# Hybrid encoder step: the FFN's up projection by seven products of block sums instead of eight block products, on equal token groups

## The chip, the cores and the metric

The kernel runs on one core of a Trainium2 chip. The metric is the device time of one execution in microseconds (us). A core has TensorE (PE; PEld is its weight load), VectorE (DVE), ScalarE (ACT) and GpSimd (POOL), all of which read and write the on-chip memory SBUF; TensorE writes its sums to PSUM, which the others read. SyncE (SP) issues the DMAs.

## What is computed

One layer of a streaming encoder over 2048 prompt tokens and 32 sample tokens, model width 1024, in float32:

```python
n = rmsnorm(x, g_mix);  z = n @ w_in                  # attention and gated linear attention (GLA)
h = x + concat(attention, gla) @ w_out                # output projection
y = h + relu(rmsnorm(h, g_ffn) @ w_up)^2 @ w_down     # FFN: w_up 1024 x 4096, w_down 4096 x 1024
```

The change concerns the last line, above all `rmsnorm(h) @ w_up`.

## The kernel before

Three phases follow one another: attention, GLA, and from about 780 us on `ffn_phase` with the output projection and the FFN. Activations lie feature-major: 128 features on the partitions, tokens along the free axis.

Each large product runs in a split precision: a float32 matrix is written as a pair of float32r parts, high and low (`h`, `l`), and `mm3` issues three matmuls for one block product (high by high, high by low, low by high). The high part is written by ScalarE as a rounded copy, the low one is the difference, taken by VectorE (of activations) or GpSimd (of weights, L198).

The FFN takes the tokens in three pieces of two groups: 288 + 256 tokens, then 384 + 384 twice. For each piece:

1. The output projection `op` of both groups, 8 blocks of 128 features f, each 8 x 3 matmuls (`project_out`). VectorE adds it to the residual stream `y` (L1048), ScalarE squares the sum (L1050) and VectorE adds the squares up in `acc` (L1052). With group 1's blocks, group 0's normed input is split: ScalarE writes `h0h` (L1038), VectorE `h0l` (L1039); group 1's `h1h`, `h1l` follow within block 0. `token_scale` is a task woven into TensorE's order: one matmul `ss` with a matrix of ones sums `acc` over the partitions, then VectorE computes 1/sqrt on a full 128 x N tile `rb` (L993, L170 to L175).
2. 16 blocks b of 256 FFN columns. `weights(b)` loads and splits four tiles of 128x1024: two of w_up (`wu`), two of w_down (`wd`). `up(b, gi)` computes two halves mi of 128 columns, each 8 feature blocks x 3 = 24 matmuls (tile `up`); on the result VectorE takes relu and the scale (L1083, PSUM to `rr`), ScalarE squares it into `uh` (L1085), VectorE squares it too (L1086) and takes the low part `ul` (L1087). `down(b, gi)` has 8 features x 2 halves x 3 = 48 matmuls (tile `dn`), and VectorE adds each of the 8 results to `y` (L1104). So a block has 96 up and 96 down matmuls. The order on TensorE is up(b, 0), down(b-1, 1), up(b, 1), down(b, 0): group 1 runs half a block behind, and while u of one group is being finished, TensorE works on the other. The u tiles have two buffers.

TensorE's program order is the order of the code (`_pe` chains the instructions; `tick` weaves spawned tasks in). The orders on the other engines are the tile scheduler's.

Of the kernel before, what the change touches and what calls it, by code (L numbers as in the profile page):

```python
# [9 lines left out]
F32 = mybir.dt.float32  # L10
# [18 lines left out]
class Builder:  # L29
    def __init__(self, ctx, tc, a, o, nt=NT, ffn=True):  # L30
# [19 lines left out]
        # the tensor engine's program order: GEMMs, with tasks woven in  # L50
# [6 lines left out]
    # tile index nt stands for the sample's 32 tokens  # L57
# [12 lines left out]
    def tok_pair(self, name, n):  # L70
        """A float32r pair [P, 8, n]."""
        return tuple(
            self.tok.tile([P, KB * 288], F32R, tag="tok", name=f"{name}{x}")[:, : KB * n].rearrange(
                "p (k t) -> p k t", k=KB
            )
            for x in "hl"
        )
# [7 lines left out]
    # ------------------------------------------------ tensor engine: order and tasks  # L85
# [6 lines left out]
    def mm(self, out, lhsT, rhs, start, stop):  # L92
        n = 1
        for d in rhs.shape[1:]:
            n *= d
        m = 1
        for d in lhsT.shape[1:]:
            m *= d
        if rhs.dtype == F32R:
            ns = max(n / 2.4 + 2.5, 0.835 * m)  # L100
        else:
            ns = 4 * n / 2.4 + 5
            if m <= 64:  # beside one in the other half of the columns
                ns /= 2
        self._pe(self.T.matmul(out, lhsT, rhs, start=start, stop=stop), ns)  # L105
# [5 lines left out]
    def table(self, *args, **kw):  # L111
        """An activation of the GLA phase: in program order, so that its functions change tables seldom."""
# [25 lines left out]
    def finish(self, *tasks):  # L138
        """Run the tasks (all of them, without arguments) to their ends."""
# [11 lines left out]
    def gemm(self, ps, lh, ll, rh, rl):  # L151
        """ps = (lh + ll).T @ (rh + rl) over 8 blocks of the contraction."""
# [25 lines left out]
    def rms(self, xt, sq, r, name):  # L178
        """rsqrt(mean(xt^2) + eps), row by row; sq takes the squares."""
# [5 lines left out]
    def split_weight(self, src, hi, lo, hi_eng="act", lo_eng="pool", parts=1):  # L185
        """Load a piece [128, k, c] of a weight, k * c <= 1024, and write it as a float32r pair."""
# [13 lines left out]
    def cols_pair(self, w, c0, name, engs=(("act", "pool"), ("act", "pool")), k0=0, nk=KB):  # L200
        """Rows 128*k0 : 128*(k0+nk), columns c0 : c0+2048/nk of a [P, 8, *] weight view as a float32r pair."""
# [19 lines left out]
    # ------------------------------------------------ attention  # L221
    def attention_phase(self):
# [3 lines left out]
        with ExitStack() as ctx:  # L226
# [17 lines left out]
            def front(t, xT=None):  # L244
                """x * g, feature-major, as a float32r pair."""
# [21 lines left out]
            def scales(t, x=None):  # L267
                """1 / rms of each token, by which its products are scaled."""
# [4 lines left out]
            def store(t):  # L273
                """The pair and the scales, for the GLA phase."""
# [11 lines left out]
            S.activation(self.rstd[:, :1], self.ones[:, :1], AF.Square)  # L286
# [6 lines left out]
            # k, v and, beside them, the forget gate's low-rank part  # L293
# [10 lines left out]
            gq, gk, snk, snks = self.gq, self.gk, self.snk, self.snks  # L304
# [52 lines left out]
            def project_gate(t):  # L357
                """The gate's projection, kept for the GLA phase."""
# [7 lines left out]
            def softmax_tail(rsum, negm, snk_b, n, name):  # L366
                """1 / (rsum + exp(sink - max))"""
# [7 lines left out]
            def transposed_qk(t, qk, kn, ca):  # L375
# [7 lines left out]
                caT = wk.tile([16, P], F32, tag="caT", name=f"caT_{t}")  # L383
# [4 lines left out]
            def attend_sample(qk, kn, v, ca):  # L388
# [48 lines left out]
                aT = self.const.tile([P, 4, P], F32, tag="mo", name="aT_s", bufs=2)  # L437
# [3 lines left out]
            def attend(t, qk, kn, v, ca):  # L441
# [22 lines left out]
                for ch in range(2):  # L464
# [46 lines left out]
                for ch in range(2):  # L511
                    ops = []
                    for vt, a0, m in parts[ch]:
# [5 lines left out]
                        else:  # L519
                            # both heads' 64 keys on the partitions  # L520
# [15 lines left out]
                aT = self.const.tile([P, 4, P], F32, tag="mo", name=f"aT_{t}", bufs=2)  # L536
# [6 lines left out]
            # the first two tiles go together, so that there is work while the weights come in  # L543
# [25 lines left out]
            # the GLA phase's first projections run beside the last tiles' attention  # L569
# [11 lines left out]
    # ------------------------------------------------ gated linear attention  # L581
    GLA_ENG = (("act", "pool"), ("dve", "dve"))

    def load_gla_consts(self):
        a, c, Q, V = self.a, self.mid, self.Q, self.V
        ct = lambda shape, name, dt=F32: c.tile(shape, dt, tag=name, name=name, bufs=1)
        masks, d0 = ct([P, 7, 32], "masks", I32), ct([P, 544], "d0")
# [39 lines left out]
    def decay(self, h, tail=None):  # L627
        """The running sums of log sigmoid(ca @ w_alpha + b_alpha), restarted at each tile."""
# [4 lines left out]
        resets = d0[:, :288] if h == 0 else d0[:, 288:]  # L633
# [23 lines left out]
    def gla_phase(self):  # L657
        tc, a, V, S, G, Q = self.tc, self.a, self.V, self.S, self.G, self.Q
        nt = self.nt
        with ExitStack() as ctx:  # L660
# [3 lines left out]
            masks, d0, wal, bal, one, ones = self.gla_consts  # L664
            St = {}
# [13 lines left out]
            def reach(n, s):  # L679
                """Run the n-th tile's task to the end of a stage (1: diagonal, 2: scores, 3: outputs, 4: all)."""  # L680
# [4 lines left out]
            def gates(h):  # L685
                """silu(gate) * g_gla_out"""
                for t in halves[h]:
# [6 lines left out]
                    G.tensor_tensor(out=gv, in0=gv, in1=self.ggla[:r].unsqueeze(1).broadcast_to([r, 4, P]), op=ALU.mult)  # L694
# [54 lines left out]
            def gla_tile(n, t, off, qg, kg, cc):  # L749
# [55 lines left out]
                # the diagonal of the scores  # L805
# [16 lines left out]
                # level by level, the pairs that a block's middle parts  # L822
# [42 lines left out]
                # outputs, token by token, and the state after these tokens  # L865
# [29 lines left out]
                # norm per head, gate, transpose  # L895
# [16 lines left out]
                gT = self.const.tile([P, 4, P], F32, tag="mo", name=f"gT_{t}", bufs=2)  # L912
# [16 lines left out]
    # ------------------------------------------------ output projection and FFN  # L929
# [4 lines left out]
    def load_mix(self, g, pair):  # L934
        """The attention's and the GLA's outputs for tiles g, feature-major, as a float32r pair."""
        off = 0
        for t in g:
            r = self.rows(t)
            m = self.io_tile(f"m_{t}")[:, : KB * r].rearrange("p (k t) -> p k t", k=KB)
            self.Q.dma_start(m, self.mixT[t])  # L940
            hi, lo = (x[:, :, off : off + r] for x in pair)
            self.S.activation(hi, m, AF.Copy)
            self.V.tensor_tensor(out=lo, in0=m, in1=hi.bitcast(F32), op=ALU.subtract)
            off += r
        return off

    def project_out(self, f, N, pair, wo, name):
        """Features 128*f : 128*(f+1) of the output projection."""
# [3 lines left out]
        self.gemm(ps, lambda kb: w(kb, 0), lambda kb: w(kb, 1), lambda kb: pair[0][:, kb, :N], lambda kb: pair[1][:, kb, :N])  # L952
        return ps

    def prepare_ffn(self, part):
# [5 lines left out]
        # the first tiles' output projection runs beside the last tiles' GLA  # L961
        if part < 3:
            self.mix.append(self.tok_pair(f"m{part - 1}", 288))
            self.load_mix(self.pieces[0][part - 1], self.mix[-1])
            return
        self.wo += self.load_wout(0, (1,), (("act", "pool"), ("dve", "dve")))
        self.op0, N = [], sum(self.rows(t) for t in self.pieces[0][0])
# [6 lines left out]

    def ffn_phase(self, pieces):
# [279 lines left out]
```

## Time and profile before

| | |
|---|---|
| median of three runs | 2415.68 us (2412.44 to 2417.94) |
| the profiled execution: span | 2416.1 us, mean granted TensorE clock 0.982 |
| TensorE busy | 2318.7 us, 14981 matmuls |
| VectorE, ScalarE, GpSimd busy | 1543.2, 717.9, 746.2 us |

The profiled execution's own time is its span, from the first to the last instruction. Busy times of different engines overlap; which of them sets the time is read from the chain of waits that ended last. In a group's row of the profile stand the line, the engine, what is written from what, the shape and the count, then busy us and mean ns of one, then the idle time before it and its releaser.

### The profile page before, as it was taken

The page shows a single profiled execution, that of the slowest core. Times are in us where ns is not written, and L with a number is a line of the kernel's source. Part 1 is how long each engine was busy: PE and PEld are TensorE (multiplying, and loading weights), DVE is VectorE, ACT ScalarE, POOL GpSimd, SP SyncE. Part 2 cuts the span into 40 slices and gives each one's busy share as a digit, 9 for nine tenths or more (in the row PEclk, how much of TensorE's full clock was granted, in tenths as well). Part 3 has the DMA queues.
Part 4 walks back from the last instruction along what each step waited for, and adds up shares of the span by engine and source line. Part 5 has one row for each costly group of instructions (what it writes and reads, how often), then busy time and mean ns, then how long its engine had stood idle before and what let it go on. Part 6 is the DMA issues. An engine that isn't in the chain of part 4 may idle for free.

```text
span 2416.1 us, 37655 instructions
## 1 busy us (share of the span) xinstructions
PE 2318.7 (96%) x14981; PEld 2183.3 (90%) x14981; DVE 1543.2 (64%) x3403; ACT 717.9 (30%) x1397; POOL 746.2 (31%) x636
## 2 busy tenths in 40 slices
PE   6999999889978899999999999999999999999999
PEld 5777777777868899999999999999999999999999
DVE  6766666999997866666656555554565655555554
ACT  3554444545443322222323111111122311111110
POOL 3222235332430343434313223332231322333220
PEclk9999999999989899999999999999999999999999
DMA  9764564223224332323432122222252212221211
GB/s 212 149 132 107 124 170 123 62 66 99 66 77 135 97 105 71 106 71 119 153 97 71 61 62 70 70 62 61 80 167 84 73 56 68 70 71 56 60 33 53
DMA packets 199279, 221.55 MB, mean 92 GB/s; under 512 B 18064, under 2 KB 163040, under 8 KB 199104
## 3 DMA queue, kind: packets, MB, share of 16 engines
q1 hardware_dynamic: 199104, 219.15, 32.7%
q8 instruction: 118, 1.93, 0.4%
q14 instruction: 57, 0.47, 0.1%
HBM read 180.21 MB, written 38.91 MB: 91 GB/s over the span
## 4 chain that ended last, share of the span: by engine, by line
PE 79%; DVE 13%; DMA 4%; issue 2%; ACT 2%; POOL 1%; SPq 0%; DVEq 0%; POOLq 0%; ACTq 0%
PE dn L105 29%; PE up L105 29%; PE op L105 7%; PE zq L105 4%; PE zr L105 3%; DVE Qb L793 3%; PE zkv L105 2%; DVE AT L858 1%; PE O L105 1%; DVE E L799 1%; DMA xT1a<-in_xT_prompt 1%; PE S L105 1%; PE zv L105 1%; DMA stage<-in_w_in 1%; DMA nTl<-nT_0l 1%
## 5 line engine op out<-in xcount | busy, mean ns | idle before, releaser
L1104 DVE TENSOR_TENSOR y<-y,dn 128x384 f32<-128x384 f32 (+2 forms) x768 | 379.5, 511 | 157.7 <-PE dn L105 155.5
L1083 DVE SCALAR_TENSOR_TENSOR rr<-up,rb 128x384 f32<-128x384 f32 (+1 forms) x192 | 99.4, 518 | 385.5 <-PE up L105 385.1
L1085 ACT ACTIVATE uh<-rr 128x384 fp32r<-128x384 f32 (+1 forms) x192 | 93.7, 489 | 716.6 <-DVE rr L1083 716.6
L1086 DVE TENSOR_TENSOR rr<-rr 128x384 f32<-128x384 f32 (+1 forms) x192 | 173.5, 905 | 66.1 <-ACT uh L1085 65.7
L1087 DVE TENSOR_TENSOR ul<-rr,uh 128x384 fp32r<-128x384 f32 (+1 forms) x192 | 175.4, 915 | 3.2
L793 DVE TENSOR_TENSOR Qb<-qg,E 64x128 f32<-64x128 f32 (+1 forms) x234 | 86.2, 368 | 7.2 <-ACT E L113 4.0
L694 POOL TENSOR_TENSOR g<-g,packed 128x512 f32<-128x512 f32 (+1 forms) x17 | 22.7, 1340 | 168.5 <-ACT g L113 168.5
L858 DVE COPY_PREDICATED AT<-masks,A 64x128 f32<-64x128 int32 (+1 forms) x197 | 67.5, 342 | 8.4 <-ACT AT L851 3.4
L494 ACT ACTIVATE P<-S,negm 128x192 f32<-128x192 f32 (+2 forms) x128 | 51.5, 417 | 52.2 <-DVE negm L489 35.4
L1048 DVE TENSOR_TENSOR y<-y,op 128x384 f32<-128x384 f32 (+2 forms) x48 | 24.0, 512 | 67.3 <-PE op L105 67.3
L783 POOL TENSOR_TENSOR E<-cc 128x128 f32<-128x128 f32 (+1 forms) x117 | 48.5, 414 | 17.0 <-PE A L105 8.9
L784 POOL TENSOR_TENSOR E<-cc 128x128 f32<-128x128 f32 (+1 forms) x117 | 51.9, 444 | 0.0
L488 DVE TENSOR_REDUCE mx<-S 128x2 f32<-128x384 f32 (+2 forms) x64 | 32.5, 533 | 24.3 <-PE S L105 24.2
L507 POOL TENSOR_TENSOR P<-P,es 128x512 f32<-128x512 f32 x15 | 15.6, 1041 | 98.1 <-DVE es L372 42.0
L198 POOL TENSOR_TENSOR wu_0l<-stage,wu_0h 128x1024 fp32r<-128x1024 f32 x3 | 7.5, 2483 | 121.5 <-ACT wu_0h L194 121.5
L105 PE MATMUL go<-Sp,Qc 128*128 128x256 f32 x60 | 22.0, 454 | 23.5 <-DVE Sp L891 23.5
L1050 ACT ACTIVATE sq<-y 128x384 f32<-128x384 f32 (+2 forms) x42 | 20.5, 490 | 80.2 <-DVE y L1048 74.2
L799 DVE TENSOR_TENSOR E<-E,kg 128x1024 f32<-128x1024 f32 (+2 forms) x34 | 40.4, 1205 | 0.1
L113 ACT ACTIVATE E<-E 128x1024 f32<-128x1024 f32 (+2 forms) x34 | 33.7, 1009 | 18.5 <-POOL E L774 12.2
L105 PEld LDWEIGHTS A<-Qb,E 128*64 128x64 f32 (+1 forms) x852 | 32.2, 149 | 6.9 <-issue 3.1
L815 ACT ACTIVATE AT<-packed,dg 128x128 f32<-128x128 f32 (+1 forms) x68 | 21.3, 384 | 57.4 <-DVE dg L813 57.4
L105 PE MATMUL dn<-uh,wd_0h 128*128 128x384 f32 (+2 forms) x96 | 33.2, 345 | 5.4 <-ACT uh L1085 5.4
(1147 smaller groups left out, 8651.3 us busy)
## 6 DMA issues: line engine op xcount, KB each, us to landing
stage<-in_w_up SPq DMA_DIRECT2D x96, 512.0 KB, 3.8
stage<-in_w_down SPq DMA_DIRECT2D x96, 512.0 KB, 3.6
stage<-in_w_out SPq DMA_DIRECT2D x24, 512.0 KB, 4.7
xT1a<-in_xT_prompt SPq DMA_DIRECT2D x16, 512.0 KB, 6.7
stage<-in_w_in SPq DMA_DIRECT2D x16, 512.0 KB, 13.1
x1a<-in_x_prompt SPq DMA_DIRECT2D x16, 512.0 KB, 5.1
m<-mixT SPq DMA_DIRECT2D x16, 512.0 KB, 4.8
y<-in_xT_prompt SPq DMA_DIRECT2D x16, 512.0 KB, 6.7
```

The costliest lines, as they stand in the source:

```text
L105: self._pe(self.T.matmul(out, lhsT, rhs, start=start, stop=stop), ns)
L494: S.activation(Pt[:, u, :n], sp[:, jp], AF.Exp, bias=negm[:, ch, u : u + 1], scale=0.125, accum_out=rsum[:, ch, u : u + 1],)
L783: G.tensor_tensor(out=e5[:, :, :, 0, :], in0=ref, in1=c5[:, :, :, 0, :], op=ALU.subtract)
L784: G.tensor_tensor(out=e5[:, :, :, 1, :], in0=c5[:, :, :, 1, :], in1=ref, op=ALU.subtract)
L793: (G if li % 4 < 0 else V).tensor_tensor(out=Qt[hp, li, :, hh, : L // 2].rearrange("q p (n m) -> q p n m", m=m), in0=q[hp].rearrange("q p ...
L799: V.tensor_tensor(out=E[:, :ng, :, :L], in0=E[:, :ng, :, :L], in1=k.unsqueeze(1).broadcast_to([P, ng, 2, L]), op=ALU.mult)
L858: V.copy_predicated(dst, mk.unsqueeze(1).broadcast_to([L // nh, 4, w // m, m]), src)
L1083: V.scalar_tensor_tensor(out=rr, in0=ps, scalar=0.0, in1=rbs[gi], op0=ALU.max, op1=ALU.mult)
L1085: last_s = S.activation(uhs, rr, AF.Square)
L1086: V.tensor_tensor(out=rr, in0=rr, in1=rr, op=ALU.mult)
L1087: last_v = V.tensor_tensor(out=ul[:, mi, :], in0=rr, in1=uhs.bitcast(F32), op=ALU.subtract)
L1104: V.tensor_tensor(out=yg[:, f, :], in0=yg[:, f, :], in1=ps, op=ALU.add)
```

## The change

**Pieces.** The groups of a piece get equal size: 320 + 320 tokens, then 360 + 360 twice. The groups no longer fall on multiples of 128 tokens, so their loads and stores are cut in more parts.

**Up projection.** For a block of 256 columns and a piece's two groups, the product is seen as 2 x 2 blocks: A by halves of the columns and of the 1024 features (4 feature blocks each), B by halves of the features and by group. Seven products of sums (Winograd's form of Strassen's scheme) give the four results: P0 = A11 B11, P1 = A12 B21, P2 = S1 T1, P3 = S2 T2, P4 = S3 T3, P5 = A22 T4, P6 = S4 B22. Each is 4 x 3 = 12 matmuls, 84 a block. The results are c0 = P0 + P1, and with r2 = P0 + P3, r0 = r2 + P4: c1 = r0 - P5, r0 + r1 (r1 = P2), and r2 + r1 + P6. VectorE forms them; `finished` then takes relu and scale (VectorE), the square and its rounded copy (ScalarE) and the low part (VectorE). `uh0`, `ul0` and `uh1`, `ul1` are the two column halves of group 0, 2 and 3 those of group 1.

**Weight sums.** `up_weights` forms S1 to S4 on GpSimd: with the seven low parts, eleven GpSimd operations of 128x512 and, for w_down, two of 128x1024 a block, where there were four of 128x1024. ScalarE writes seven high parts of 128x512 and two of 128x1024.

**Token sums.** At a piece's start `combine` forms T1, T2, T4 beside group 1's output projection, and T3 and B22 follow. Every sum and its pair must be there before its product in block 0.

**Order.** up(b) has all seven products, then down(b, 0), which starts with the first halves of four features, then down(b, 1). Nothing runs half a block behind. u, r0 to r2, the T and B tiles have one buffer.

**Token scale.** `token_scale` now sums into a small tile (120 x 3 or 80 x 4), takes the rsqrt on that, and spreads it by matmuls `rb` to `cb`. In TensorE's order `ss` of group 1 stands ahead of P1 of block 0, and its `rb` ahead of P2.

```diff
-        if nt == 16:
-            self.pieces = [[[0, 1, nt], [2, 3]], [[4, 5, 6], [7, 8, 9]], [[10, 11, 12], [13, 14, 15]]]
...
+        for n in (320, 360, 360):
...
+            def up_weights(b, name):
...
+                names = ("A11", "A12", "S1", "S2", "S4", "S3", "A22")
...
+                def pair(x, src):
+                    h, l = ws[x]
+                    S.activation(h, src, AF.Copy)
+                    G.tensor_tensor(out=l, in0=src, in1=f32(h), op=ALU.subtract)
...
+                pair("A11", A(1, 1))
+                pair("A12", A(1, 2))
+                pair("A22", A(2, 2))
+                tt(A(2, 2), A(2, 1), A(2, 2), ALU.add)
+                tt(A(2, 1), A(1, 1), A(2, 1), ALU.subtract)
+                tt(A(1, 1), A(2, 2), A(1, 1), ALU.subtract)
+                pair("S1", A(2, 2))
+                tt(A(1, 2), A(1, 2), A(1, 1), ALU.subtract)
+                pair("S2", A(1, 1))
+                pair("S3", A(2, 1))
+                pair("S4", A(1, 2))
...
+                def finished(i, x):
+                    V.scalar_tensor_tensor(out=x, in0=x, scalar=0.0, in1=cb[i // 2], op0=ALU.max, op1=ALU.mult)
+                    S.activation(x, x, AF.Square)
+                    S.activation(uh[i], x, AF.Copy)
+                    V.tensor_tensor(out=ul[i], in0=x, in1=f32(uh[i]), op=ALU.subtract)
...
+                    S.activation(r0, product(0, "A11", "B11"), AF.Copy)
+                    ps = product(1, "A12", "B21")
+                    if b == 0:
+                        self.finish(*tasks)
+                    tt(c0, ps, r0)
+                    finished(0, c0)
+                    S.activation(r1, product(2, "S1", "T1"), AF.Copy)
+                    ps = product(3, "S2", "T2")
+                    tt(r2, ps, r0)
+                    ps = product(4, "S3", "T3")
+                    tt(r0, ps, r2)
+                    tt(r2, r2, r1)
+                    ps = product(5, "A22", "T4")
+                    tt(c1, r0, ps, ALU.subtract)
+                    finished(1, c1)
+                    ps = product(6, "S4", "B22")
+                    tt(r0, r0, r1)
+                    finished(3, r0)
+                    tt(r2, ps, r2)
+                    finished(2, r2)
...
+                for k in range(H):
+                    f = H + k
+                    t0 = (r[1], r[2], tmp[:, :N], tmp[:, N : 2 * N])[k]
+                    S.activation(t0, y[1][:, k, :], AF.Copy, scale=g(k))
+                    V.scalar_tensor_tensor(out=t0, in0=y[1][:, f, :], scalar=g(f), in1=t0, op0=ALU.mult, op1=ALU.subtract)
+                    split("T3", k, t0)
+                for k in range(H):
+                    scaled("B22", k, 1, H + k)
...
-                for b in range(NF):
-                    last_s, last_v = up(b, 0)
...
-                        down(b - 1, 1)
...
-                    up(b, 1)
...
-                    down(b, 0)
...
+                for b in range(NF):
+                    last = b + 1 == NF
+                    up(b)
...
+                    down(b, 0, 4)
...
+                    down(b, 1)
```

What moves on the engines shows at three places. In the rows, `dn_1_7_0_0` is down's tile for piece 1, block 7, group 0, feature 0, the number behind a name is the buffer's, and the bracket names the engines or DMA queues that are waited for. First VectorE in the middle of the second piece, block 7, as group 0's u is finished, before:

```order
L1083 SCALAR_TENSOR_TENSOR rr_1_7_0_0_15916<-up_1_7_0_0_15891,rb1_0_13734 128x384 [waits PE_49]
L1086 TENSOR_TENSOR rr_1_7_0_0_15916<-rr_1_7_0_0_15916 128x384 [waits Activation_49]
L1087 TENSOR_TENSOR ul_1_7_0_15890<-rr_1_7_0_0_15916,uh_1_7_0_15889 128x384 [waits DVE_49]
L1083 SCALAR_TENSOR_TENSOR rr_1_7_0_1_15946<-up_1_7_0_1_15921,rb1_0_13734 128x384 [waits PE_49]
L1104 TENSOR_TENSOR y1_1_13327<-y1_1_13327,dn_1_6_1_0_15951 128x384 [waits PE_49]
L1086 TENSOR_TENSOR rr_1_7_0_1_15946<-rr_1_7_0_1_15946 128x384 [waits Activation_49]
L1104 TENSOR_TENSOR y1_1_13327<-y1_1_13327,dn_1_6_1_1_15959 128x384 [waits PE_49]
L1087 TENSOR_TENSOR ul_1_7_0_15890<-rr_1_7_0_1_15946,uh_1_7_0_15889 128x384 [waits DVE_49]
```

And now, from c1 on (`PA22T4` is P5, `PS4B22` P6):

```order
L1170 TENSOR_TENSOR c1_7_16363<-r0_8740,PA22T4_1_7_16439 128x360 [waits PE_49]
L1150 SCALAR_TENSOR_TENSOR c1_7_16363<-c1_7_16363,cb0_8738 128x360 [waits DVE_49]
L1170 TENSOR_TENSOR r0_8740<-r0_8740,r1_8741 128x360
L1150 SCALAR_TENSOR_TENSOR r0_8740<-r0_8740,cb1_8739 128x360 [waits DVE_49]
L1170 TENSOR_TENSOR r2_8754<-PS4B22_1_7_16457,r2_8754 128x360 [waits PE_49]
L1153 TENSOR_TENSOR ul1_8735<-c1_7_16363,uh1_8731 128x360 [waits Activation_49]
L1150 SCALAR_TENSOR_TENSOR r2_8754<-r2_8754,cb1_8739 128x360 [waits DVE_49]
L1207 TENSOR_TENSOR y0_8742<-y0_8742,dn_1_7_0_0_16516 128x360 [waits PE_49]
```

Before, each `ul` came two steps behind its L1083, with y additions of the other group between. Now the additions of group 0 wait behind the sums, and `ul1` stands behind r0 + r1, its relu and r2 + P6.

Second, GpSimd in the same piece, the weights of block 8, before and then now (`stage` tiles hold the raw weights; L1067 is `pair`'s low part, L1069 a sum):

```order
L198 TENSOR_TENSOR wu1_8l_16016<-stage_16017,wu1_8h_16015 128x1024 [waits DMAHW1_49,PE_49,Activation_49]
L198 TENSOR_TENSOR wu1_8l_16016<-stage_16021,wu1_8h_16015 128x1024 [waits DMAHW2_49,Activation_49]
L198 TENSOR_TENSOR wd1_8l_16026<-stage_16027,wd1_8h_16025 128x1024 [waits DMAHW3_49,PE_49,Activation_49]
L198 TENSOR_TENSOR wd1_8l_16026<-stage_16031,wd1_8h_16025 128x1024 [waits DMAHW4_49,Activation_49]
L198 TENSOR_TENSOR wu1_9l_16288<-stage_16289,wu1_9h_16287 128x1024 [waits DMAHW5_49,PE_49,Activation_49]
```

```order
L1067 TENSOR_TENSOR wu1_8_0_16484<-stage_16480,wu1_8_0_16484 128x512 [waits DMAHW3_49,PE_49,Activation_49]
L1067 TENSOR_TENSOR wu1_8_0_16484<-stage_16482,wu1_8_0_16484 128x512 [waits DMAHW4_49,Activation_49]
L1067 TENSOR_TENSOR wu1_8_3_16487<-stage_16482,wu1_8_3_16487 128x512 [waits PE_49,Activation_49]
L1069 TENSOR_TENSOR stage_16482<-stage_16480,stage_16482 128x4x128 [waits Pool_49]
L1069 TENSOR_TENSOR stage_16480<-stage_16480 128x4x128 [waits Pool_49]
L1067 TENSOR_TENSOR wu1_8_1_16485<-stage_16482,wu1_8_1_16485 128x512 [waits PE_49,Activation_49]
L1069 TENSOR_TENSOR stage_16480<-stage_16482,stage_16480 128x4x128 [waits Pool_49]
L1067 TENSOR_TENSOR wu1_8_2_16486<-stage_16480,wu1_8_2_16486 128x512 [waits Activation_49]
L198 TENSOR_TENSOR wd1_8l_16507<-stage_16508,wd1_8h_16506 128x1024 [waits DMAHW5_49,PE_49,Activation_49]
L1069 TENSOR_TENSOR stage_16482<-stage_16482,stage_16480 128x4x128 [waits Pool_49]
L198 TENSOR_TENSOR wd1_8l_16507<-stage_16512,wd1_8h_16506 128x1024 [waits DMAHW6_49,Activation_49]
L1067 TENSOR_TENSOR wu1_8_1_16485<-stage_16480,wu1_8_1_16485 128x512 [waits Activation_49]
```

The four operations of a block (the fifth row is the next block's) have become thirteen (the last, L1067 for S4, follows), in a chain: the sums wait for the low parts that read the same raw tile.

Third, TensorE at the start of the second piece, around group 1's `ss`, before and then now:

```order
L105 MATMUL dn_1_0_0_1_14100<-ul_1_0_0_14019,wd1_0h_14008 128x384
L105 MATMUL dn_1_0_0_1_14100<-uh_1_0_0_14018,wd1_0l_14009 128x384
L105 MATMUL ss_1_1_14104<-acc1_1_13735,ones128_179 128x384
L105 MATMUL dn_1_0_0_2_14119<-uh_1_0_0_14018,wd1_0h_14008 128x384
L105 MATMUL dn_1_0_0_2_14119<-ul_1_0_0_14019,wd1_0h_14008 128x384
```

```order
L105 MATMUL PA11B11_1_0_14349<-B11l_8751,wu1_0_0_14001 128x360
L105 MATMUL PA11B11_1_0_14349<-B11h_8750,wu1_0_0_14001 128x360
L105 MATMUL ss_1_1_14381<-ones1_179,sums1_1_13772 120x1 [waits DVE_49]
L105 MATMUL ss_1_1_14381<-ones1_179,sums1_1_13772 120x1 x2
L105 MATMUL PA12B21_1_0_14401<-B21h_8752,wu1_0_0_14001 128x360 [waits Activation_49]
L105 MATMUL PA12B21_1_0_14401<-B21l_8753,wu1_0_0_14001 128x360
```

`ss_1_1` stood inside block 0's down projection of group 0, without a wait of its own; now it stands between P0 and P1 and waits for VectorE. On VectorE the last rows of the piece's sums that come ahead of it, and the first behind it, are:

```order
L175 SCALAR_TENSOR_TENSOR rsq_y_y1_0_14359<-rsq_q_y1_0_14360,rsq_y_y1_0_14359 120x3 [waits DVE_49]
L1122 SCALAR_TENSOR_TENSOR tmp1_13773<-y1_8743,packed_177,tmp1_13773 128x360 [waits Activation_49]
L1137 TENSOR_TENSOR sums1_1_13772<-sums1_1_13772 128x360 [waits Activation_49]
L1123 SCALAR_TENSOR_TENSOR tmp1_13773<-y0_8742,packed_177,tmp1_13773 128x360 [waits DVE_49]
L1125 TENSOR_TENSOR tmp1_13773<-tmp1_13773 128x360 [waits DVE_49]
L1137 TENSOR_TENSOR sums1_1_13772<-sums1_1_13772 128x360 [waits Activation_49]
L1100 TENSOR_TENSOR T2l_8749<-tmp1_13773,T2h_8748 128x360 [waits Activation_49]
L1100 TENSOR_TENSOR T4l_8745<-tmp1_13773,T4h_8744 128x360 [waits Activation_49]
L1122 SCALAR_TENSOR_TENSOR tmp1_13773<-y1_8743,packed_177,tmp1_13773 128x360 [waits Activation_49]
L1044 TENSOR_SCALAR msy_1_1_14385<-ss_1_1_14381 120x3 [waits PE_49]
```

The last of the `sums1_1` rows (L1137) completes `acc`, behind T1's low part and a T2 and T4 in the making; L1044 takes up `ss_1_1`.

More of the change, by code (lines that the diff above doesn't have):

```diff
@@ new lines, in load_y, with next_mix, token_scale @@
+                return yt
+            def next_mix(pi, gi):
+                n = self.size(pieces[pi][gi])
+                names = (("B11", "B21"), ("T3", "B22"))[gi]
+                hi, lo = ([view(tok[x][y], n) for x in names] for y in range(2))
+                self.load_mix(pieces[pi][gi], hi, lo)
+                mix[gi] = lambda kb, x: (hi, lo)[x][kb // H][:, kb % H, :]
+            def token_scale(name, N, acc, cb):
+                n = next(n for n in range(1, N) if N % n == 0 and N // n <= P)
+                r = N // n
+                ps = self.ps_s(f"ss_{name}")[:r, :n]
+                for c in range(n):
+                    self.mm(ps[:, c : c + 1], acc[:, c * r : (c + 1) * r], self.ones, True, True)
+                ms = self.small.tile([P, 4], F32, tag="msy", name=f"msy_{name}")[:r, :n]
+                V.tensor_scalar(out=ms, in0=ps, scalar1=1.0 / D, scalar2=EPS, op0=ALU.mult, op1=ALU.add)
+                rs = self.rsqrt(ms, r, n, f"y{name}")
+                yield 3000
+                rb = self.ps_m(f"rb_{name}")[:, :N]
+                for c in range(n):
+                    self.mm(rb[:, c * r : (c + 1) * r], rs[:, c : c + 1].broadcast_to([r, P]), self.ident[:r, :r], True, True)
+                S.activation(cb, rb, AF.Copy)
@@ L1090, in down @@
-                def down(b, gi, split=0):
-                    N, yg, (uh, ul), (dnh, dnl) = sizes[gi], ys[gi], us.pop((b, gi)), ws[b][1]
+                        if gi:
+                            scaled(("B11", "B21")[f // H], f % H, 0, f)
+                            combine(f)
+                    tasks.append(token_scale(f"{pi}_{gi}", N, acc, cb[gi]))
+                    if gi == 0:
+                        with tc.issue_after(self.y_loads if pi == 0 else self.last_load):
+                            ws[0] = weights(pi, 0)
@@ L1093, in down @@
+                def down(b, gi, first=0):
+                    yg, (dnh, dnl) = y[gi], ws[b][1]
                     pss = {}
-                    order = [(f, 0) for f in range(split)] + [(f, 1) for f in range(split)]
-                    for f, mi in order + [(f, mi) for f in range(split, KB) for mi in range(2)]:
+                    order = [(f, 0) for f in range(first)] + [(f, 1) for f in range(first)]
+                    for f, mi in order + [(f, mi) for f in range(first, KB) for mi in range(2)]:
```

299 lines of the change are left out of this document (159 added, 140 removed).

## Prediction

> **What bounds the kernel now.** I read the page first (engines, then the chain that ended last).
>
> ```profile
> span 2416.1 us, 37655 instructions
> PE 2318.7 (96%) x14981; PEld 2183.3 (90%) x14981; DVE 1543.2 (64%) x3403; ACT 717.9 (30%) x1397; POOL 746.2 (31%) x636
> PE 79%; DVE 13%; DMA 4%; issue 2%; ACT 2%; POOL 1%; SPq 0%; DVEq 0%; POOLq 0%; ACTq 0%
> ```
>
> TensorE carries 79% of the chain, VectorE 13%. The change touches only the FFN, so next comes the chain from 860 us to the end.
>
> ```profile
> by line: PE dn L105 44.3%; PE up L105 43.9%; PE op L105 8.6%; DVE h1l L943 0.5%; DVE ul L1087 0.5%; DVE y L1104 0.5%; DVE rr L1086 0.5%; issue 0.3%; DVE h0l L943 0.2%; PE ss L105 0.2%; DVE rr L1083 0.1%; ACT uh L1085 0.1%; ACT h0h L942 0.1%
> 895.86 6.39 PE dn L105 x48
> 902.25 6.40 PE up L105 x48
> ...
> 926.56 6.40 PE up L105 x48
> ...
> 1333.05 8.32 PE up L105 x48
> 1341.37 8.32 PE dn L105 x48
> ```
>
> There TensorE is 97% of the chain and the products follow one another without a gap. 48 matmuls take 6.40 us at 288 tokens (133.3 ns each) and 8.32 us at 384 (173.3 ns). The line through both is N/2.4 + 13.3 ns, so 163.3 ns at 360 tokens and 146.7 at 320. A block of the first piece takes 926.56 - 902.25 = 24.31 us, a block of the others 4 x 8.32 = 33.28. 16 x (24.31 + 2 x 33.28) = 1453.9 us of the span are such blocks.
>
> Second, what the engines beside TensorE do in a block (groups by shape, from 900 us on), then VectorE and GpSimd on a stretch of the second piece.
>
> ```profile
> L1104 DVE TENSOR_TENSOR y<-y,dn 128x384 f32<-128x384 f32 x512 | 273.1, 550 | 123.0 <-PE dn L105 122.0
> L1087 DVE TENSOR_TENSOR ul<-rr,uh 128x384 fp32r<-128x384 f32 x128 | 121.7, 952 | 2.1
> L1086 DVE TENSOR_TENSOR rr<-rr 128x384 f32<-128x384 f32 x128 | 105.5, 826 | 46.2 <-ACT uh L1085 46.0
> L1083 DVE SCALAR_TENSOR_TENSOR rr<-up,rb 128x384 f32<-128x384 f32 x128 | 71.3, 557 | 306.9 <-PE up L105 306.6
> L1085 ACT ACTIVATE uh<-rr 128x384 fp32r<-128x384 f32 x128 | 66.5, 521 | 532.5 <-DVE rr L1083 532.5
> ```
>
> ```profile
> 1525.46 5.08 POOL L198 TENSOR_TENSOR wu_9l<-stage,wu_9h 128x1024 fp32r<-128x1024 f32 x2 [3.56 <-ACT wu_9h L194]
> ...
> 1527.00 1.28 DVE L1086 TENSOR_TENSOR rr<-rr 128x384 f32<-128x384 f32 x1
> 1528.21 0.54 DVE L1104 TENSOR_TENSOR y<-y,dn 128x384 f32<-128x384 f32 x1
> 1528.67 2.28 DVE L1087 TENSOR_TENSOR ul<-rr,uh 128x384 fp32r<-128x384 f32 x1
> 1530.88 1.47 DVE L1104 TENSOR_TENSOR y<-y,dn 128x384 f32<-128x384 f32 x3
> ```
>
> The same 384 columns cost VectorE 0.55 us where one operand lies in PSUM (L1104, L1083), but 0.83 and 0.95 on the mean where all lie in SBUF (L1086, L1087). The stretch shows why. While GpSimd works (1525.46 to 1530.54) the operations on SBUF alone take 1.28 and 2.28 us, and the one with a PSUM operand between them 0.54. The next rows give the size, at the start of the second piece.
>
> ```profile
> 1254.93 2.41 POOL L198 TENSOR_TENSOR wu_0l<-stage,wu_0h 128x1024 fp32r<-128x1024 f32 x1 [43.69 <-ACT wu_0h L194]
> 1257.30 2.71 POOL L198 TENSOR_TENSOR wd_0l<-stage,wd_0h 128x1024 fp32r<-128x1024 f32 x1
> ...
> 1255.01 2.74 DVE L174 SCALAR_TENSOR_TENSOR rsq<-rsq,acc 128x384 f32<-128x384 f32 x1
> 1257.67 3.41 DVE L198 TENSOR_TENSOR wu_0l<-stage,wu_0h 128x1024 fp32r<-128x1024 f32 x1
> ```
>
> L174 came 0.08 us after GpSimd's operation and ended 0.41 after its end (1257.34 to 1257.75); GpSimd's second took 2.71 instead of 2.41, since it waited for L174; L198 on VectorE waited for that. The two take turns. Now it is hidden: four GpSimd operations a block, and the second group half a block behind.
>
> **The products.** In a block, 192 matmuls become 180 (7 x 4 x 3 = 84 up, 96 down). 180 take 26.40 us at 320 tokens and 29.40 at 360; 16 x (26.40 + 2 x 29.40) = 1363.2, which is 90.7 less than 1453.9. The Trainium skill (TensorE: Matmul & The Clock Gate, Back-to-back issue gap) has N/2.4 + 2.5 ns for a lone warm matmul, and 10.8 ns less per matmul would make the gain about 85 us; the rows show 13.3 ns in this stream, and the rows are used.
>
> **What VectorE and GpSimd get.** VectorE goes from 12 operations on u a block (4 with PSUM) to 15 (5 with PSUM, so 10 on SBUF alone instead of 8), beside 16 y additions as before. GpSimd goes from four operations of 128x1024 to two of those and eleven of 128x512.
>
> ```profile
> L263 POOL TENSOR_TENSOR nT_2l<-xT1a,nT_2h x4: 1276/1289/1305, 54.6 to 63.6; 128x512 fp32r<-128x512 f32 x4
> L507 POOL TENSOR_TENSOR P<-P,es 128x512 f32<-128x512 f32 x15 | 15.6, 1041 | 98.1 <-DVE es L372 42.0 <-ACT sq L334 34.4 <-DVE mx L488 8.8
> L198 POOL TENSOR_TENSOR wd_3l<-stage,wd_3h 128x1024 fp32r<-128x1024 f32 x6 | 14.3, 2405 | 53.4 <-ACT wd_3h L194 53.4
> ```
>
> I take 1.28 us for 128x512 (L263 has the same two inputs; L507 with 1.04 is the other bound). 11 x 1.28 + 2 x 2.41 = 18.9 us a block. Turns included, GpSimd is busy most of a 29.4-us block, just while VectorE works the last products off. The second group is no longer half a block behind, so nothing covers that.
>
> I stepped one block at 360 tokens through the engines in their new order, with t = 0 at P0's start. Products end every 1.96 us: P5 at 11.76, P6 at 13.72. A VectorE step of 360 columns takes 0.53 (0.55 at 384, 24 columns less). c1 = r0 - P5 has a PSUM operand: 11.96 to 12.49. Its relu and scale, on SBUF, fall between two GpSimd operations: 13.05. r0+r1 then has to let a GpSimd operation pass, 1.28 + 0.41 less 0.2 of overlap: 14.54. The relu of r0 likewise: 16.04. r2+P6, with PSUM, 16.50. Only then comes ul1 (its uh1 was ready long before): 17.54. TensorE needs ul1 when it has done the first halves of four features (12 matmuls) and one more: 13.72 + 1.96 + 0.16 = 15.84. It waits 1.77 us with 0.07 of hand-over. At 320 tokens the need comes at 14.23, while the GpSimd operations stay as long: 2.75 us. ul2 is ready at 23.2, needed at 23.5. Sum: 16 x 2.75 + 32 x 1.77 = 100.6 us, more than the products save. The ends: without turns ul1 is ready at about 15.0 and the stall is 0; if a 128x1024 operation falls in the chain too, 1.1 us more in each of 48 blocks, 53 us. I take the walk, since its step is the one of L174.
>
> **The piece starts.** Now:
>
> ```profile
> 790.00:835.00 45.00, 37.28 (x252) 36.40 (x252) 38.30 (x64) 13.97 (x27) 17.05 (x7) 0.85 0.32 102
> 1193.00:1286.00 93.00, 88.00 (x511) 86.95 (x511) 51.57 (x77) 26.36 (x42) 24.46 (x10) 0.98 0.39 122
> 1795.00:1890.00 95.00, 91.94 (x521) 89.83 (x521) 53.96 (x80) 26.15 (x42) 22.33 (x9) 1.00 0.42 131
> L174 DVE SCALAR_TENSOR_TENSOR rsq_q_qk<-rsq_q_qk,ssqk x51: 130/170/946, 36.8 to 362.1; 128x10 f32<-128x10 f32 x48, 32x10 f32<-32x10 f32 x3
> ```
>
> The first column of engines is TensorE's busy time: it idles 7.7 + 5.0 + 3.1 = 15.8 us over the three starts. After, VectorE's order has 20 operations on SBUF (T1, T2, T3, T4, B22, acc), 12 small ones of the rsqrt and one with PSUM between the last product of the output projection and the completed acc, for which ss_1_1 waits ahead of P1: 20 x 0.445 (the pitch of steps back to back: the x3 row of L1104 has 1.47 for three, so 0.46 at 384, 0.02 less at 360) + 12 x 0.16 + 0.53 = 11.3, less P0's 1.96: 9.3 us idle. Up to the rsqrt that rb_1_1 needs ahead of P2 come 12, 12 and 1 more: 7.8 less P1's 1.96, 5.8 us. 15 us a start is the floor; the ceiling has all 18.9 us of GpSimd's first weights taking turns in it, 34. I take 20, since most of those 13 operations run earlier, beside the projection. 3 x 20 - 15.8 = +44 us. The projection's matmuls move little: 192 x (120.0 + 4 x 173.3) = 156.1 us before, 192 x (146.7 + 4 x 163.3) = 153.6 after.
>
> **The clock.**
>
> ```profile
> 792.36 1.93 issue
> 795.00:800.00 5.00, 5.00 (x32) 5.00 (x31) 4.59 (x13) 1.95 (x4) 0.00 (x0) 0.66 0.59 204
> 1194.00 0.28 PE L105 MATMUL dn<-uh,wd_15l 128*128 128x256 f32 x1
> 1198.25 0.58 PE L105 MATMUL dn<-uh,wd_15h 128*128 128x256 f32 x1 [3.97 <-DVE y L1104]
> 1198.85 0.41 PE L105 MATMUL dn<-uh,wd_15l 128*128 128x256 f32 x1
> 1202.11 0.28 PE L105 MATMUL dn<-ul,wd_15h 128*128 128x256 f32 x1
> ```
>
> After 1.93 us without a matmul the granted clock was 0.66 in the next 5 us, and after 3.97 us matmuls took 0.41 instead of 0.28 for about 3.4 us. A spell costs some 1.7 us. If half of the first piece's 2.75-us stalls set one off: +8 (0 to 27). The long idles at the starts: +2. The Trainium skill (the same page, Why this matters for your kernels) says that only gaps over about 3 us cool the clock; the 1.93-us row disagrees; by that rule the 8 would be 0.
>
> Sum: 2416.1 - 90.7 + 100.6 + 44 + 8 + 2 = 2480; the profiled execution is 0.4 us over the median (2415.68). The added clock spells are the least sure, so I say 2475.
>
> **Rivals.** (B) The seven products pay: ul1 is ready by 15.84 us after P0, because GpSimd's operations fall elsewhere or take L507's 1.04 us. Then the stall is near 0: 2416 - 90.7 + 44 + 2 = 2371 (2356 at the floor of the starts). For it: L1083 and L1104 never wait. Against it: the order keeps GpSimd without a pause there. (C) Half the stall: 2416 - 90.7 + 50 + 44 = 2420, no change. (D) A 128x1024 operation in the chain, or clock spells in most blocks: 2480 + 53 = 2533 and over. Against it: by the walk both come after ul1.
>
> **Chances.** Forecast (2435 to 2525) 0.66, B 0.19, C 0.08 (half of it within 0.2%, the rest split), D 0.07. What a measurement can tell from no change is 0.2%, 4.8 us. Faster 0.21, same 0.05, slower 0.74. The range 2370 to 2530 leaves out half of B and D's upper part.
>
> **What would show it.** Right: in the chain of after, `dn` waits for ul1 in each block, some 1.8 us at 360; the block period is 31.2 and 29.1 us; the two-SBUF steps (r0, c1, ul) average over 0.8 us, those with PSUM 0.53; at each start two TensorE idles ahead of P1 and P2, 15 us or more together. Wrong: a period of 29.4, or a c1-to-ul1 span under 4 us, makes it B.

## The result, and the profile after

The changed kernel takes 2523.78 us (median of four runs, 2519.77 to 2525.31) beside 2415.6 us before on the same chip: ratio 1.0445, 95% interval 1.043 to 1.046. That is slower, as forecast, and inside the range, but 6 us below its upper end and 1 us below that of the forecast's own band (2435 to 2525): the forecast of +59 us fell short of the +108. The engines' busy times and the chain by engine, of the changed kernel:

```profile
span 2521.1 us, 38199 instructions
PE 2272.1 (90%) x14473; PEld 2121.2 (84%) x14473; DVE 1739.3 (69%) x3657; ACT 966.1 (38%) x2035; POOL 1269.4 (50%) x1074
PE 61%; DVE 29%; ACT 3%; DMA 3%; issue 2%; POOL 1%; SPq 1%; DVEq 0%; ACTq 0%; POOLq 0%
```

TensorE is busy 46.6 us less, and VectorE has gone from 13% to 29% of the chain. One block of the second piece, as the chain of waits has it (start us, length, what):

```profile
1473.31 1.98 PE PA11B L105 x12
...
1483.21 1.99 PE PA22T L105 x12
...
1485.23 0.54 DVE c L1170
...
1485.79 0.53 DVE c L1150
1486.33 1.56 DVE r L1170
...
1487.91 1.50 DVE r L1150
1489.41 0.44 DVE r L1170
1489.85 1.09 DVE ul L1153
...
1490.99 13.93 PE dn L105 x83
1504.92 0.17 PE PA11B L105
```

From P5's end the chain leaves TensorE and runs down VectorE: c1, its relu, then r0+r1 and the relu of r0 at 1.5 us each, r2, ul1. The block lasts 1504.92 - 1473.31 = 31.61 us. The groups by shape from 860 us on tell the two kinds of step apart:

```profile
L1150 DVE SCALAR_TENSOR_TENSOR r<-r,cb 128x360 f32<-128x360 f32 x64 | 99.4, 1555 | 1.1
L1170 DVE TENSOR_TENSOR r<-r,r 128x360 f32<-128x360 f32 x64 | 76.9, 1201 | 3.2
L1170 DVE TENSOR_TENSOR r<-PS3T,r 128x360 f32<-128x360 f32 x32 | 17.0, 532 | 45.3 <-PE PS3T L105 45.3
```

Steps on SBUF alone take 1.2 to 1.6 us, the same columns with a PSUM operand 0.53. (The list of engines at the top is too wide: in these traces all of TensorE's results go to PSUM, and no GpSimd operation touches a tile that TensorE wrote.) What TensorE waited for, from 760 us to the end (us in total, times, longest):

```profile
PE dn L105 <- DVE ul L1153: 99.4, 61, 4.5
PE ss L105 <- DVE sums L1137: 47.3, 3, 18.1
PE dn L105 <- ACT uh L1152: 9.1, 5, 2.5
PE rb L105 <- DVE rsq_y_y L175: 5.8, 3, 2.6
```

Two costs, then: the wait for u in every block, and the wait for acc at each of three starts.

### The profile page after: what moved, and what is told of

The parts are those of the page before. It is cut to its first block, busy times and chain, and to the rows that moved or that the text cites. A ratio compares the mean times of both kernels' runs of the same rounds, so it can differ in the third digit from the quotient of the medians.

```text
span 2521.1 us, 38199 instructions
## 1 busy us (share of the span) xinstructions
PE 2272.1 (90%) x14473; PEld 2121.2 (84%) x14473; DVE 1739.3 (69%) x3657; ACT 966.1 (38%) x2035; POOL 1269.4 (50%) x1074
## 4 chain that ended last, share of the span: by engine, by line
PE 61%; DVE 29%; ACT 3%; DMA 3%; issue 2%; POOL 1%; SPq 1%; DVEq 0%; ACTq 0%; POOLq 0%
PE dn L105 22%; DVE r L1170 5%; PE PA12B L105 4%; PE PS1T L105 4%; PE op L105 4%; PE PS2T L105 4%; PE PS3T L105 4%; DVE ul L1153 4%; PE PA11B L105 3%; PE zq L105 3%; DVE r L1150 3%; PE zr L105 3%; DVE Qb L798 3%; PE PA22T L105 2%; DVE AT L863 2%
## 5 line engine op out<-in xcount | busy, mean ns | idle before, releaser
L1067 POOL TENSOR_TENSOR wu<-stage,wu 128x512 fp32r<-128x512 f32 x336 | 451.9, 1362 | 633.6 <-ACT wu L1066 633.5
L1207 DVE TENSOR_TENSOR y<-y,dn 128x360 f32<-128x360 f32 (+1 forms) x768 | 372.9, 509 | 162.3 <-PE dn L105 160.4
L1069 POOL TENSOR_TENSOR stage<-stage 128x512 f32<-128x512 f32 x192 | 289.6, 1508 | 7.5
L1066 ACT ACTIVATE wu<-stage 128x512 fp32r<-128x512 f32 x336 | 199.2, 621 | 118.4 <-POOL stage L1069 116.7
L1150 DVE SCALAR_TENSOR_TENSOR r<-r,cb 128x360 f32<-128x360 f32 (+1 forms) x96 | 131.8, 1375 | 1.7
L1170 DVE TENSOR_TENSOR r<-r,r 128x360 f32<-128x360 f32 (+1 forms) x96 | 122.4, 1275 | 3.8
L1153 DVE TENSOR_TENSOR ul<-r,uh 128x360 fp32r<-128x360 f32 (+1 forms) x96 | 107.1, 1117 | 7.4 <-ACT uh L1152 7.4
L105 PE MATMUL PA12B<-B21h,wu 128*128 128x360 f32 (+1 forms) x384 | 103.0, 332 | 0.0
L105 PE MATMUL PS1T<-T1h,wu 128*128 128x360 f32 (+1 forms) x384 | 100.4, 325 | 0.0
L105 PE MATMUL PA11B<-B11h,wu 128*128 128x360 f32 (+1 forms) x384 | 99.7, 321 | 0.0
```

Source lines behind the costliest of these rows:

```text
L1066: S.activation(h, src, AF.Copy)
L1067: G.tensor_tensor(out=l, in0=src, in1=f32(h), op=ALU.subtract)
L1069: tt = lambda o, x, y, op: G.tensor_tensor(out=o, in0=x, in1=y, op=op)
L1150: V.scalar_tensor_tensor(out=x, in0=x, scalar=0.0, in1=cb[i // 2], op0=ALU.max, op1=ALU.mult)
L1153: V.tensor_tensor(out=ul[i], in0=x, in1=f32(uh[i]), op=ALU.subtract)
L1170: tt = lambda out, x, y, op=ALU.add: V.tensor_tensor(out=out, in0=x, in1=y, op=op)
```

## Experiments

Ratios are to the kernel before, timed beside each run.

**1. GpSimd writes, but reads nothing.**

```diff
-                    G.tensor_tensor(out=l, in0=src, in1=f32(h), op=ALU.subtract)
+                    G.memset(f32(l), 0.0)
...
-                tt = lambda o, x, y, op: G.tensor_tensor(out=o, in0=x, in1=y, op=op)
+                tt = lambda o, x, y, op: G.memset(o, 0.001)
```

(The low parts of w_down likewise.)

> Every GpSimd operation on the FFN's weights becomes a memset of the same output: GpSimd writes as many tiles but reads nothing from SBUF (the low parts are zero and the weight sums a constant, so the products are not the reference's). Theory 'turns' (VectorE's steps on SBUF alone let a reading GpSimd operation pass): the wait for ul1 goes, block periods fall from 31.64 and 29.73 us to about 29.8 (360 tokens) and 26.8 to 27.5 (320), and the starts get a little shorter: 2400 to 2425 us. Rival 'long chain' (fifteen VectorE steps and the hops to ScalarE are too long by themselves): periods within 0.3 us of now, 2510 us or more.

2375.71 us, ratio 0.9826 (0.9807 to 0.9845), 24 us under the range of "turns". A 360-token block lasts 29.69 us, a 320-token one 27.40. The starts' waits, then the same step as above and (from 1450 to 1850 us) a memset, from the groups by shape:

```profile
PE rb L105 <- DVE rsq_y_y L175: 9.0, 4, 3.9
PE ss L105 <- DVE sums L1140: 8.5, 3, 4.2
L1153 DVE SCALAR_TENSOR_TENSOR r<-r,cb 128x360 f32<-128x360 f32 x64 | 37.9, 594 | 2.1
L1070 POOL MEMSET wu<- 128x512 f32 x77 | 38.7, 527 | 151.1 <-PE dn L105 151.1
```

The chain is as long as before and the step is back at 0.59 us, so "long chain" falls. (At 320 tokens 0.96 us a block is left over the 26.44 of experiment 2: there the square of c1 and uh1 stand behind ScalarE's copies of w_down.) A memset takes 0.53 us where the operation took 1.36, so that GpSimd is also busy less; experiment 2 leaves it its work. The surprise is the starts: the wait for ss fell from 47.3 to 8.5 us, with all of the token sums still there.

**2. GpSimd's work kept, but later.** Besides the lines shown, w_down's operations are issued behind those of w_up.

```diff
-                        ws[b + 1] = weights(pi, b + 1)
+                        gate = G.tensor_copy(out=gatem, in_=f32(ul[1])[:, :1])
+                        with tc.issue_after(gate.ins):
+                            ws[b + 1] = weights(pi, b + 1)
```

> The same work, but GpSimd's operations on the next block's weights start only when ul1 of this block is done (a copy of one column of ul1 on GpSimd ahead of them), and w_down's come last. Theory 'turns': ul1 is there about 15 us after P0, no wait for it; periods about 29.8 and 27 us, 32 x 1.9 + 16 x 2.7 = 100 us less than 2524: about 2420 us. If GpSimd then ends too late for the next block's P3 or P6, a new wait of up to 1.5 us a block on GpSimd: 2430 to 2490. Rival 'long chain': 2515 us or more.

2403.79 us, ratio 0.9938 (0.9913 to 0.9962): faster than both kernels, with every operation of the changed one in it. A block's chain, the step r0+r1 (1450 to 1850 us; 1.2 us in the changed kernel), and the starts' waits:

```profile
1557.83 1.98 PE PA11B L105 x12
...
1569.70 1.98 PE PS4B L105 x12
1571.68 15.83 PE dn L105 x96
L1175 DVE TENSOR_TENSOR r<-r,r 128x360 f32<-128x360 f32 x26 | 13.8, 530 | 1.3
PE ss L105 <- DVE sums L1142: 47.3, 3, 18.1
```

The block is TensorE from end to end, 29.69 us (26.44 at 320 tokens), and the starts are untouched. So when GpSimd reads, not how much it does, made the waits in the blocks: 32 x (31.63 - 29.69) + 16 x (29.73 - 26.44) = 115 us, against 120 measured.

**3. Group 1's token scale later in TensorE's order.**

```diff
-                tasks = [self.spawn(x, d) for x, d in zip(tasks, (0, 1500))]
+                tasks = [self.spawn(x, d) for x, d in zip(tasks, (0, 6000))]
...
+                    if b == 0:
+                        self.finish(tasks[1])
                     finished(3, r0)
```

> Group 1's sum of squares and its broadcast (ss_1, rb_1) come some 4.5 us of matmuls later in TensorE's order, and the code takes up group 1's scale only ahead of its first use in block 0. Theory 'queue ahead of ss' (TensorE waits at each start for the acc behind VectorE's token sums): the 14.6 to 18.1 us wait ahead of P1 goes, and 9 to 12 us of it come back ahead of P2 to P4, where T1 to T4 are waited for: 12 to 20 us less in all, 2504 to 2512 us. Rival 'VectorE's whole backlog': what is waited for is T3, last in the queue anyway, and the time moves by less than 5 us.

2537.99 us, ratio 1.0504 (1.0486 to 1.0523): 14 us slower than the changed kernel, which neither theory had. The waits of all starts, that for rb at the second piece's start alone, and part of the chain there:

```profile
PE rb L105 <- DVE rsq_y_y L175: 34.5, 5, 11.8
PE ss L105 <- DVE sums L1137: 7.0, 2, 3.8
...
PE rb L105 <- DVE rsq_y_y L175: 11.4, 2, 11.1
...
1386.17 1.74 DVE rsq_y_y L170
...
1388.35 2.23 DVE rsq_y_y L171
...
1419.71 0.17 DVE rsq_q_y L173
```

Most of the wait for ss went, and TensorE stops instead at the next thing in its order, group 0's rb: 11.0 to 11.8 us at each start, where group 1's rb, the one that was moved, waits 0.3 at the second. Group 0's rsqrt lies scattered among the sums in VectorE's queue, from 1386 to 1399 us. Its steps on 120 x 3 numbers take 1.7 and 2.2 us beside GpSimd's operations on block 0's w_down (1385.5 to 1390.6 us), where the last ones of group 1, with GpSimd done, take 0.17. In the changed kernel, too, group 0's rsqrt ends only at 1396.6 us, 2.8 us before the wait for ss does, so moving ss alone could win little.

**4. Eight products, everything else of the change kept.**

```diff
-                names = ("A11", "A12", "S1", "S2", "S4", "S3", "A22")
+                names = ("A11", "A12", "A21", "A22")
...
+                    for i, x in enumerate((c0, c1, r0, r2)):
+                        gi, m = divmod(i, 2)
...
+                        for j, t in enumerate((("B11", "B21"), ("T1", "B22"))[gi]):
```

> The new groups, order, single buffers and token scale stay, but each of the four results is the ordinary product over eight feature blocks (192 matmuls a block, no sums of weights or tokens; GpSimd has four operations of 128x512 and two of 128x1024). Theory 'turns': no wait for ul1, periods about 192 x 0.165 = 31.7 and 192 x 0.1475 = 28.3 us, 21 us less in the blocks, and 20 to 35 us less at the starts, where the token sums fall away: 2465 to 2485 us. Rival 'the order costs' (nothing half a block behind any more): the waits stay, the periods become 33 us or more, and the time is 2530 us or more.

2425.63 us, ratio 1.0036 (1.0022 to 1.0051). From the chain and the waits:

```profile
1557.08 15.84 PE P L105 x96
1572.92 15.83 PE dn L105 x96
PE ss L105 <- DVE sums L1129: 3.1, 1, 3.1
```

No waits in the blocks (31.67 and 28.20 us), so the order and the single buffers do no harm by themselves. The blocks sum to 16 x 28.20 + 32 x 31.67 = 1465 us. That is 11 over the 1453.9 of the kernel before, with as many matmuls, so the new groups cost about what this version loses to it. It is 23 under the changed kernel's 1488; the other 75 of the 98 us lie at the starts, more than twice what was expected, and the time is 39 us under the range of "turns".

**5. GpSimd's operations in halves, no gate.**

```diff
+                    for ks in (slice(0, 2), slice(2, 4)):
+                        G.tensor_tensor(out=l[:, ks], in0=src[:, ks], in1=f32(h)[:, ks], op=ALU.subtract)
```

> The changed kernel with each of GpSimd's eleven 128x512 operations a block cut into two of 128x256: the same bytes and the same start, no gate. Theory 'turns' (a VectorE step on SBUF lets the one running GpSimd operation pass): a step waits for about 0.65 to 0.7 us instead of 1.28, the three steps ahead of ul1 give back about 0.6 us each, ul1 comes about 15.9 us after P0 and the wait for it nearly goes; the second wait of the 320-token blocks (uh2 behind ScalarE's copies, 1.0 us) may stay: 2420 to 2450 us. Rival 'share' (what counts is how much of the time GpSimd reads SBUF, which does not fall): the wait stays, 2510 us or more.

2444.25 us, ratio 1.0112 (1.0089 to 1.0135), as "turns" said. The same steps in a block, GpSimd's group, and the starts:

```profile
1596.48 1.00 DVE r L1174
...
1597.51 0.95 DVE r L1154
...
L1068 POOL TENSOR_TENSOR wu<-stage,wu 128x256 fp32r<-128x256 f32 x639 | 513.9, 830 | 422.2 <-ACT wu L1066 422.2
PE ss L105 <- DVE sums L1141: 47.1, 3, 17.7
```

The steps fall from 1.5 to 1.0 us, though GpSimd is busy longer (2 x 0.83 for 1.36), and the block to 30.47 us (31.63 in whole operations). "Share" falls. But the wait did not nearly go: 0.78 us a block is left over the 29.69 without a wait. The starts did not move.

**6. Gate and halves.** The edits of 2 and 5 together.

> The gated kernel with GpSimd's 128x512 operations in halves. In the blocks nothing is left to win (periods 29.69 and 26.44 us). Theory 'turns at the starts too': VectorE's queue ahead of ss gets shorter by 3 to 8 us a start, 2380 to 2397 us. Rival 'ss waits for ScalarE and the sums themselves': within 4 us of the gated kernel's 2404.

2411.97 us, ratio 0.9984 (0.9971 to 0.9998): 8 us slower than the gate alone, against both. The wait for ss stays at 47.3 us, so "turns at the starts too" falls. The 360-token blocks stay at 29.69, the 320-token ones lengthen to 27.22. From a chain there, and GpSimd on the same stretch:

```profile
1034.23 4.64 DVE c L1159
...
1033.77 4.75 POOL L198 TENSOR_TENSOR wd_7l<-stage,wd_7h 128x1024 fp32r<-128x1024 f32 x2
```

GpSimd's list is longer now and ends 8.5 us after the next block's P0 starts, not 6.6 as with the gate alone. The relu of c0 waits for both w_down operations in a row; with the gate alone it took 2.81 us, and TensorE had no wait from it. 16 x (27.22 - 26.44) = 12 us, about the difference by the ratios (0.0046 of 2416, 11 us).

**7. The changed kernel without token sums.**

```diff
-                            combine(f)
...
-                        th, tl = T[t]
+                        th, tl = T[{"T1": "B11", "T2": "B21", "T3": "B22", "T4": "B11"}.get(t, t)]
```

> The changed kernel without the sums of tokens: T1 to T4 are not formed, and their products take B11, B21 and B22 instead (the FFN's results are not the reference's); weight sums, order and token scale stay. Theory 'VectorE's queue' (the token sums on VectorE ahead of the acc make TensorE wait at each start): the waits for ss and rb fall from 53 us to under 15, 2468 to 2490 us; the waits for ul1 in the blocks stay. Rival 'first weights' (GpSimd's sums for block 0, and ScalarE behind them, set the start): the waits stay, within 10 us of 2524.

2489.36 us, ratio 1.032 (1.0293 to 1.0348): 34 us less than the changed kernel, just in the first range, but the wait for ss was to fall under 15. The waits, and ScalarE at the second piece's start:

```profile
PE dn L105 <- DVE ul L1152: 93.9, 62, 2.2
PE ss L105 <- DVE sums L1137: 28.1, 3, 11.2
1363.00 0.63 ACT L1066 ACTIVATE wu<-stage 128x512 fp32r<-128x512 f32 x1 [1.86 <-POOL stage L1069]
1364.26 0.90 ACT L1135 ACTIVATE sums<-y 128x360 f32<-128x360 f32 x2 [0.62 <-POOL wu L1067]
```

Both theories hold in part. ScalarE stands before the high parts of the first weights until GpSimd has formed their sums, and the squares for acc are behind them in its queue: the first y of group 1 is there at 1341.6 us, and its square starts at 1364.26.

**8. Gate, and block 0 by eight products.** The edit of 2 is in it, and group 1's scale comes later in TensorE's order.

```diff
+                    if b == 0:
+                        up_plain()
+                        token_sums()
+                    else:
+                        up(b)
```

> The gated kernel (GpSimd's weights behind ul1) with block 0 of each piece by the ordinary eight block products: 12 matmuls more a piece, but the weight sums fall away there and T1 to T4 are formed after block 0's products in the code instead of ahead of them. Theory 'queue ahead of ss': the waits for ss (47 us in three starts) and rb (6 us) shrink to a few us, and 6 us of matmuls come back: 2355 to 2375 us. Rival 'same work later': VectorE's sums hold up block 0's y additions and through them TensorE as long as before, 2395 to 2410 us.

2379.23 us, ratio 0.9847 (0.9821 to 0.9873), between the two theories, and the fastest version that leaves nothing out. No wait for ss is left in its list; in its place are smaller ones, above all:

```profile
PE rb L105 <- DVE rsq_y_y L175: 11.7, 3, 5.2
PE dn L105 <- DVE ul L1164: 5.4, 3, 4.1
```

## Why the prediction was right, and where it was short

By spans the change costs 2521.1 - 2416.1 = 105.0 us.

| term | forecast | measured | from |
|---|---|---|---|
| products | -90.7 | -80.8 | periods without a wait (experiment 2): 16 x (26.44 - 24.31) + 32 x (29.69 - 33.28) |
| waits in the blocks | +100.6 | +115 | periods of the changed kernel less those of experiment 2 |
| starts and clock | +54 | +71 | what is left |

The way and the mechanism were right. The size was 41 us short by the prediction's own sum (2480 for 2521.1), and all three terms missed to the same side.

**The turns were right.** At 360 tokens the walk had c1 at 12.49, r0+r1 at 14.54, its relu at 16.04 and ul1 at 17.54; the chain above has 12.46, 14.57, 16.10 and 17.63 after P0's start. Experiments 1, 2 and 5 show the cause: reading, its time and its grain. The Trainium skill (SBUF — State Buffer, Who interferes with whom) says that a VectorE instruction with two SBUF inputs contends with a GpSimd instruction that reads SBUF, and not with one that only writes: experiment 1 agrees, 0.59 us beside memsets for 1.56 beside reads.

**Products mis-sized.** The line through 288 and 384 tokens gave 163.3 ns at 360; measured are 1.98/12 = 165 ns, in experiment 4 too (15.84/96). Over 32 x 180 matmuls that is the 10 us.

**The second wait at 320 tokens was missed.** The sum of the waits was about right there (2.75 for 1.72 + 1.04), by luck, since the walk had the whole at ul1. The chain has a second one, where uh2 stands behind the w_down copies on ScalarE and ul2 then lets a w_down operation on GpSimd pass:

```profile
915.77 1.89 ACT wd_3h L194 x2
917.66 0.37 ACT uh L1152
...
918.06 1.79 DVE ul L1153
...
917.11 2.39 POOL L198 TENSOR_TENSOR wd_3l<-stage,wd_3h 128x1024 fp32r<-128x1024 f32 x1
```

The 14 us over the forecast are 0.54 us a block at 320 tokens (3.29 for 2.75) and 0.17 at 360 (1.94 for 1.77). They are what a wait costs besides its listed length. TensorE around the wait of the block above:

```profile
1488.99 0.33 PE L105 MATMUL dn<-uh,wd_2h 128*128 128x360 f32 x1
1490.99 0.43 PE L105 MATMUL dn<-ul,wd_2h 128*128 128x360 f32 x1 [1.67 <-DVE ul L1153]
1491.26 0.33 PE L105 MATMUL dn<-uh,wd_2l 128*128 128x360 f32 x1
```

The list counts from the end of the last record, 0.33 us long, though matmuls start 0.165 us apart in the stream, and the first matmul after the wait is followed only 0.27 us later. So 1.67 + 0.165 + 0.105 = 1.94 us at 360 tokens. At 320 two waits make 1.72 + 1.04 + 2 x 0.27 = 3.3.

**The clock in the blocks was wrong.** The 8 us for half-clock spells did not come (by the prediction's own figures it should have been 8 spells of 1.7 us, 13.6): the granted clock is 1.00 through the 320-token blocks, as their row shows ahead of one of a start.

```profile
890.00:919.70 29.70, 26.97 (x180) 26.45 (x180) 19.64 (x32) 10.07 (x19) 19.69 (x14) 1.00 0.22 72
...
1400.75 3.81 PE PA12B L105 x12
```

The failed step is the single stall of 2.75 us. It came as two, 1.72 and 1.04, both shorter than the 1.93-us idle that the prediction had read, so that reading was not put to the test in the blocks. By the Trainium skill (TensorE: Matmul & The Clock Gate, Why this matters for your kernels) gaps under about 3 us should set nothing off. The waits in the blocks agree, but the first piece's last block does not: after a wait of 2.45 us and one of 1.80 right behind it the granted clock was 0.50 until 1306.5 us, and matmuls started 0.27 us apart instead of 0.147. At the starts the clock falls too: P1 took 3.81 us instead of 1.98 after the 14.7-us wait.

**The starts were mis-sized, 44 + 2 for 71.** The waits for ss and rb come to 53 us where 60 were forecast, before the 15.8 of the kernel before are taken off. That makes 37 of the 71. An estimate from the gaps between matmuls' starts at the three starts gives the rest: about 14 us for longer waits in the first and last blocks (up to 4.5 us, by the list above), about 11 for the small matmuls of ss and rb themselves, which the sum had at nothing, and about 8 for more matmuls at half clock (P1 above), where the sum had 2.

That VectorE's queue sets the start was half the truth. Without token sums 28 us of the wait for ss stay (experiment 7); with them, but with memsets on GpSimd, 8.5 stay (experiment 1). So GpSimd's work on the first weights, which the term had mostly beside the projection, has the larger part, by turns with VectorE or through ScalarE's queue. How much each adds isn't separated, since the order on VectorE moves with each edit.

**The rivals.** B (ul1 in time) needed GpSimd's operations elsewhere; experiment 2 put them there and gained 120 us. But it came out at 2404 and not at 2371, for the 10 us of the products and the dearer starts. C did not occur. D did in a part: at 320 tokens a 128x1024 operation is in the chain, at ul2, behind ul1 as the walk had it, but TensorE waits there too. The chances of the same and slower also add up to 0.04 and 0.75, not 0.05 and 0.74.

## What to carry to other kernels

When an edit takes work from the bound engine and gives it to two whose reads of SBUF hold each other up (here 1.56 us beside reads, 0.59 beside memsets), step one iteration through their queues, and count each step on SBUF alone as about one operation of the neighbour longer. The remedy is then when and in what grain the neighbour reads, not less work: one dependence that held GpSimd back until the last urgent VectorE step was worth 120 us here. And price the start of a stage by its own queues; here, with the clock, it cost 71 us, almost as much as the 81 that the seven products save.

## What the runs showed of the hardware that was not expected

- VectorE steps on 120 x 3 numbers (0.17 us) also let a GpSimd operation pass, and then take 1.7 and 2.2 us (experiment 3).
- The two don't always take turns: in experiment 6 a relu on VectorE waited for two w_down operations in a row, 4.64 us, though it came during the first.
- Waits of 1.04 to 1.72 us in the blocks left the granted clock at 1.00; after one of 2.45 us it was 0.50.
- Cutting a GpSimd operation in two cost time on GpSimd, 2 x 0.83 us for 1.36, and still freed VectorE.
